# Seven block products for eight in the second load of each token-major group, in a two-layer fp32 trunk

## The chip, the cores and the metric

The kernel runs on one core of one Trainium2 chip. The core has five engines with a queue each: TensorE (PE, matrix multiplication, whose loading of stationary blocks is listed as PEld), VectorE (DVE), ScalarE (ACT), GpSimd (POOL) and SyncE (SP, which here issues the loads). PE writes its sums to eight PSUM banks of 128 x 512 fp32. The metric is the device time of one execution in microseconds (us); the median over runs is compared.

## The reference

256 tokens of width 2048 pass through an mLSTM layer and a differential-attention layer, each followed by a gated feed-forward part with a short convolution, then a last RMS norm. Weights and sums are float32. Cut to its products, with `rms_norm`, gates and softmax as their names say:

```python
# layer 0
proj = rms_norm(h, a_norm) @ w_in                 # 2048 -> q 1024, k 1024, v 2048, o 2048, gates 16
hm = mlstm_chunkwise(q, k, v, i_pre, log_f)       # 8 heads, v of width 256 a head
h = h + (rms_norm(hm, w_hnorm) * sigmoid(o)) @ w_out             # 2048 x 2048
h = h + conv_ffn(rms_norm(h, f_norm[0]), w_up, ..., w_down)      # 2048 -> 2 x 5632 -> 2048
# layer 1
k, v = split(rms_norm(h, kv_norm) @ w_kv)         # 2048 -> 2048 + 2048, k rotated
q = rotated(rms_norm(h, b_norm) @ w_q)
pd = softmax(q1 k1) - lam * softmax(q2 k2)        # causal, 8 heads
h = h + (rms_norm(pd @ v, subln) * (1 - lambda_init)) @ w_o      # 2048 x 2048
h = h + conv_ffn(rms_norm(h, f_norm[1]), w_up, ..., w_down)
return rms_norm(h, final_norm)
```

## The kernel before, in words

**Products in halves.** Every fp32 operand is split in a high part h (a copy rounded by ACT to the type PE reads) and a low part l (the rest, by DVE); a product is three matmuls, xh wh + xl wh + xh wl. Weights come as loads of 1 MB, four k-tiles of 128 rows by 512 columns, into four slots ("raw"). Half a load at a time ACT makes h (line 376) and DVE l (line 377), into one of five slots ("w2"). Activations are split once, when they are made.

**Token-major products.** v, o, w_out, attention v, w_o and w_down have tokens on the output's partitions. `gemm_tokens` (products on line 437) goes through groups of 512 columns; a group has 16 k-tiles (w_down more) and two PSUM banks, a for tokens 0 to 127 and b for 128 to 255. Two k-tiles are 12 matmuls of 128x512 (columns of weights moving past a stationary 128x128 block of x). After the last k-tile `evac` takes the banks.

**Seven products for eight.** `gemm_sevenths` (products on line 493) treats one load of a group, at the k-tile named in `at`, otherwise: two k-tiles, two halves of tokens and two halves of columns form a 2 x 2 product of blocks, which Strassen's scheme in Winograd's form makes with seven block products in place of eight. A block product is three matmuls of 128x256, so four k-tiles take 42 of these in place of 24 of 128x512. The scheme needs differences of weight blocks (`sevenths`, lines 449 to 451, into a "raw" slot), seven blocks split rather than four (lines 458 and 459, tiles of 3 x 256 and 4 x 256 columns), mixtures of the x blocks (`mix`, lines 531 to 537; `mix_again` for x that was split before, its first step on line 551), and sums of the products: some go straight into a and b, the rest into two further banks c and d, which are added up at the end of the group, by `mixed_up` (lines 559 to 565) into a and b, or by `mixed_in` (lines 572 to 579) into the residual stream. The remaining k-tiles of the group are plain (line 503).

Before the change that load is the third of the group (k-tile 8, `OUT_AT`), and seven groups have it: o 1 and 2, w_out 1 to 3, w_o 2 and 3. All groups of v and attention v are plain. w_down has its own places (`MIXED`).

**Banks.** Four of the eight banks are the pool `acc_ps`, which holds a and b of two successive groups; four are `sm_ps`, for all small products (scores, values, turns, columns of parameters) and, before, for c and d.

**What sets the order.** The code runs once and records instructions; a list scheduler then gives each engine its queue, by priority in program order and its own idea of what is ready. `tick()` stands after each two k-tiles, and `later(n, f)` puts f after n further ticks: so the small work of a head is spread between the large products. In attention, the keys of the eight heads come from a product by pairs of k-tiles; after each head's keys `rotated` (lines 936 to 941) multiplies and rotates them on DVE and POOL, `softmax` makes the scores on PE (955 to 957), maxima (959), exponentials and the weights `pc` (966 to 970), and `turned` transposes them on PE (977) for ACT and DVE to split (`pt`, 321 and 323). The last heads' part of this falls into the first groups of attention v. In mLSTM the same holds of `weights`, `values` and `scaled`; there the norm's inverse root is computed by POOL in 12 small instructions (lines 279 to 282), and ACT's scaling on line 348 waits for it.

## Time and profile before

| | |
|---|---|
| median of 3 runs | 2253.62 us (2253.61 to 2253.67) |
| profiled execution | 2253.21 us |
| span of its instructions | 2251.4 us |
| PE busy | 2239.6 us (99%) |
| DVE busy | 1789.7 us (79%) |
| ACT busy | 1292.0 us (57%) |
| POOL busy | 125.0 us (6%) |
| DMA | 419.04 MB, 186 GB/s over the span |

All durations come from the profiled execution. Rows of groups read: line, engine, operation, written tile <- read tiles, shape, number; then busy time in all in us, mean of one in ns, and the engine's idle time just before them with what ended it. Rows of the timeline give start and length in us, both from the span's start. Rows of waits give who waited for whom: us in all, times, longest. The row "PEclk" gives the clock granted to PE in tenths, in 40 slices of the span.

### The profile page before, as it was taken

To read this page: it belongs to the slowest core of one execution; us is meant where nothing else is said; L and a number is where in the kernel's file an instruction comes from. 1 tells how busy PE (TensorE), PEld (TensorE's weight loads), DVE (VectorE), ACT (ScalarE), POOL (GpSimd) and SP (SyncE) were. 2 spreads that over 40 slices of the span, in tenths; PEclk is the share of its full clock that TensorE was granted. 3 is DMA by queue.
4 is the path that set the end of the run, shared out by engine and by line. 5 is a ranking of instruction groups with operands and counts; after the bars stand their busy time and mean duration, and the time that the engine had idled before them with its cause. 6 is when DMAs were issued, how large, how long until landed. Compare 5 with 4: busy or idle time off the path is not lost.

```text
span 2251.4 us, 33430 instructions
## 1 busy us (share of the span) xinstructions
PE 2239.6 (99%) x12843; PEld 1954.1 (87%) x12843; DVE 1789.7 (79%) x2964; ACT 1292.0 (57%) x1994; POOL 125.0 (6%) x305
## 2 busy tenths in 40 slices
PE   9999999999999999999999999999999999999998
PEld 9888888888888888888888888888888888888888
DVE  5756778887888877879998885677877988778896
ACT  5456655655555555656654556566555555556554
POOL 0014200000000000000022103200000000000000
PEclk9999999999999999999999999999999999999999
DMA  7554546555555755545566555465555457555464
GB/s 265 188 169 157 166 171 205 192 191 187 187 170 179 242 187 187 187 150 203 189 208 194 163 167 169 150 206 187 187 187 187 156 191 239 191 189 191 146 215 150
DMA packets 325348, 419.04 MB, mean 186 GB/s; under 512 B 9070, under 2 KB 238788, under 8 KB 325188
## 3 DMA queue, kind: packets, MB, share of 16 engines
q1 hardware_dynamic: 325156, 416.89, 56.4%
q8 instruction: 101, 1.65, 0.3%
q14 instruction: 59, 0.48, 0.1%
q10 hardware_dynamic: 32, 0.01, 0.0%
HBM read 414.77 MB, written 2.10 MB: 185 GB/s over the span
## 4 chain that ended last, share of the span: by engine, by line
PE 97%; DVE 1%; POOL 1%; issue 1%; ACT 0%; DMA 0%; DVEq 0%; SPq 0%; POOLq 0%
PE acc L411 54%; PE acc L503 16%; PE acc L437 12%; PE mix L493 6%; PE acc L493 4%; PE acc L634 2%; PE acc L521 1%; PE val_ps L335 1%; PE turn_ps L231 1%; PE as_ps L955 0%; DVE w L377 0%; POOL rs_u L279 0%; POOL rs_u L280 0%; DMA pos_i<-in_positions_dram 0%; POOL rs_u L281 0%
## 5 line engine op out<-in xcount | busy, mean ns | idle before, releaser
L377 DVE TENSOR_TENSOR w<-raw,w 128x1024 fp32r<-128x1024 f32 x679 | 825.9, 1220 | 280.1 <-ACT w L376 277.5
L376 ACT ACTIVATE w<-raw 128x1024 fp32r<-128x1024 f32 x679 | 713.9, 1058 | 491.7 <-PE acc L411 324.8
L411 PE MATMUL acc<-x_f,w 128*128 128x512 f32 (+1 forms) x5632 | 988.1, 337 | 0.0
L411 PEld LDWEIGHTS acc<-x_f,w 128*128 128x128 f32 x5632 | 861.7, 188 | 123.2
L503 PE MATMUL acc<-w,hid 128*128 128x512 f32 x1080 | 268.2, 394 | 0.0
L503 PEld LDWEIGHTS acc<-w,hid 128*128 128x128 f32 x1080 | 195.4, 188 | 39.0
L411 PE MATMUL acc<-x_at,w 128*128 128x512 f32 (+1 forms) x1024 | 182.1, 338 | 0.0
L411 PEld LDWEIGHTS acc<-x_at,w 128*128 128x128 f32 x1024 | 156.8, 188 | 22.2 <-issue 0.3
L458 ACT ACTIVATE w<-diff 128x1024 fp32r<-128x1024 f32 x89 | 94.1, 1057 | 111.1 <-DVE diff L451 81.7
L417 ACT ACTIVATE low<-acc 128x256 f32<-128x256 f32 x216 | 79.3, 386 | 135.4 <-PE acc L411 132.6
L459 DVE TENSOR_TENSOR w<-diff,w 128x1024 fp32r<-128x1024 f32 x89 | 108.7, 1221 | 40.9 <-ACT w L458 40.3
L437 PE MATMUL acc<-w,x_a 128*128 128x512 f32 x576 | 138.0, 396 | 0.0
L437 PEld LDWEIGHTS acc<-w,x_a 128*128 128x128 f32 x576 | 106.8, 188 | 24.2
L493 PE MATMUL mix<-w,mix 128*128 128x256 f32 x801 | 119.3, 281 | 0.0
L418 DVE TENSOR_TENSOR acc<-acc,low 128x256 f32<-128x256 f32 x216 | 84.5, 430 | 37.7 <-ACT low L417 37.3
L493 PEld LDWEIGHTS mix<-w,mix 128*128 128x128 f32 x801 | 107.0, 188 | 2.4 <-DVE w L459 0.2
L848 ACT ACTIVATE c<-u,conv 128x256 f32<-128x256 f32 x176 | 98.2, 593 | 5.5 <-DVE u L846 5.2
L939 POOL TENSOR_TENSOR sw<-sw,sin_t 32x256 f32<-32x256 f32 x32 | 42.0, 1328 | 1033.8 <-DVE sw L938 1022.5
L458 ACT ACTIVATE w<-raw 128x768 fp32r<-128x768 f32 x89 | 74.7, 840 | 37.9 <-PE acc L503 27.4
L437 PE MATMUL acc<-w,x_at 128*128 128x512 f32 x384 | 91.8, 396 | 0.0
L459 DVE TENSOR_TENSOR w<-raw,w 128x768 fp32r<-128x768 f32 x89 | 84.6, 951 | 2.8 <-ACT w L458 2.7
L493 PE MATMUL acc<-w,hid 128*128 128x256 f32 x450 | 86.3, 281 | 0.0
(302 smaller groups left out, 2320.4 us busy)
## 6 DMA issues: line engine op xcount, KB each, us to landing
raw<-in_w_up_dram SPq DMA_DIRECT2D x176, 1024.0 KB
raw<-in_w_down_dram SPq DMA_DIRECT2D x79, 1024.0 KB
raw<-in_m_w_in_dram SPq DMA_DIRECT2D x46, 1024.0 KB
raw<-in_w_kv_dram SPq DMA_DIRECT2D x32, 1024.0 KB
raw<-in_m_w_out_dram SPq DMA_DIRECT2D x16, 1024.0 KB
raw<-in_w_q_dram SPq DMA_DIRECT2D x16, 1024.0 KB
raw<-in_w_o_dram SPq DMA_DIRECT2D x16, 1024.0 KB
raw<-in_w_down_dram SPq DMA_DIRECT2D x15, 512.0 KB
```

The source lines that it names most:

```text
L376: act.activation(w2[:, :hc, 0], part, AF.Copy)
L377: dve.tensor_tensor(w2[:, :hc, 1], part, w2[:, :hc, 0].bitcast(F32), op=ALU.subtract)
L411: pe.matmul(to, a, b, start=(k == 0 and o == 0), stop=(k == kn - 1 and o == len(ops) - 1))
L417: act.activation(low, p[:, T:], AF.Copy)
L418: dve.tensor_tensor(p[:, :T], p[:, :T], low, op=ALU.add)
L437: pe.matmul(ps[t], a[:, s], b, start=(k == 0 and o == 0), stop=(k == kn - 1 and o == 2))
L458: act.activation(w2[:, :m, 0], src, AF.Copy)
L459: dve.tensor_tensor(w2[:, :m, 1], src, w2[:, :m, 0].bitcast(F32), op=ALU.subtract)
L493: pe.matmul(to, u, v, start=start and o == 0, stop=end and o == 2 and to is not a and to is not b, skip_group_check=True)
L503: pe.matmul(ps, u[:, s], v, start=(k0 + i == 0 and o == 0), stop=(k0 + i == kn - 1 and o == 2), skip_group_check=True)
L634: pe.matmul(ps[j], a, b, start=(k == 0 and o == 0 and j % 2 == 0), stop=(k == KD - 1 and o == 2), skip_group_check=True)
L848: act.activation(c, u, AF.Identity, bias=cw[:, 3, f:f + 1], scale=cw[:, 2, f:f + 1])
```

## The change

Five things, in 18 groups now: all of mLSTM v, mLSTM o, w_out and attention v, and groups 2 and 3 of w_o.

- `OUT_AT` is (4, 6): the load with seven products is the second of the group (k-tiles 4 to 7).
- v, all of o, group 0 of w_out and attention v use `gemm_sevenths`. For v and o the mixtures of x are made ahead of v rather than ahead of o; attention v makes its own from its normed x.
- With the new argument `mid`, c and d come from `acc_ps`.
- Directly behind the products of that load, within the group, `mid` adds them up: `mixed_in` into the residual stream, or `mixed_sums` into two SBUF tiles.
- At the end of the group `mixed_up` adds these tiles to a and b, two additions of 128x512. `mixed_up` before did both steps at the end.

w_down keeps its scheme, with c and d in `sm_ps`.

```diff
--- before.py
+++ after.py
@@ -37,7 +37,7 @@
 G = 512
 NG = D // G
 RAW = 4
-OUT_AT = (8, 10)
+OUT_AT = (4, 6)
 MIXED = (4, 12, 20)
 HL = 5
 WARM, WARM_X = 28, 24
@@ -461,7 +461,8 @@
             pairs.append(out)
         return pairs
 
-    def gemm_sevenths(xs, mixed, w, col0, groups, evac, at):
+    def gemm_sevenths(xs, mixed, w, col0, groups, evac, at, mid=None):
+
 
 
         kn, raws = len(xs), {}
@@ -472,7 +473,10 @@
             while k0 < kn:
                 if k0 in at:
                     if c is None:
-                        c, d = small_ps("mix"), small_ps("mix")
+                        if mid is None:
+                            c, d = small_ps("mix"), small_ps("mix")
+                        else:
+                            c, d = (acc_ps.tile([P, 2 * T], F32, tag="acc", name="mix") for _ in range(2))
                     parts = sevenths(w, col0 + g * G, k0, min(2, (kn - k0) // 2))
                     for p, (b1, b2, b3, t1, t3, t2, t4) in enumerate(parts):
                         k = k0 + 2 * p
@@ -493,6 +497,8 @@
                                 pe.matmul(to, u, v, start=start and o == 0, stop=end and o == 2 and to is not a and to is not b, skip_group_check=True)
                         if p < len(parts) - 1:
                             tick()
+                    if mid is not None and k0 == at[-1]:
+                        sums = mid(g, (c, d))
                     k0 += 4
                 else:
                     for i, (wh, wl) in enumerate(granule(w, col0 + g * G, G, k0, kn, raws, g)):
@@ -503,7 +509,7 @@
                                 pe.matmul(ps, u[:, s], v, start=(k0 + i == 0 and o == 0), stop=(k0 + i == kn - 1 and o == 2), skip_group_check=True)
                     k0 += 2
                 tick()
-            evac(g, (a, b), (c, d))
+            evac(g, (a, b), (c, d) if mid is None else sums)
 
     def gemm_by_tokens(xs, w, col0, evac):
 
@@ -551,9 +557,9 @@
             dve.tensor_tensor(c, h.bitcast(F32), l.bitcast(F32), op=ALU.add)
         return mix(pair)
 
-    def mixed_up(ps, mix):
-
-        (a, b), (c, d) = ps, mix
+    def mixed_sums(g, mix):
+
+        c, d = mix
         u = tmp("mx")
         x, y = block(F32, "mixed_a"), block(F32, "mixed_b")
         act.activation(x[1], c[:, :T], AF.Copy)
@@ -561,8 +567,11 @@
         dve.tensor_tensor(y[1], d[:, T:], u, op=ALU.add)
         dve.tensor_tensor(x[0], d[:, :T], u, op=ALU.add)
         dve.tensor_tensor(y[0], d[:, :T], y[1], op=ALU.add)
-        dve.tensor_tensor(a, a, x[2], op=ALU.add)
-        dve.tensor_tensor(b, b, y[2], op=ALU.add)
+        return x[2], y[2]
+
+    def mixed_up(ps, sums):
+        for p, x in zip(ps, sums):
+            dve.tensor_tensor(p, p, x, op=ALU.add)
 
     def mixed_in(g, mix):
 
@@ -748,7 +757,8 @@
             for n in range(2):
                 dve.tensor_tensor(k[2 * j + n], ps[n], norm.r, op=ALU.mult)
 
-        def evac_v(g, ps):
+        def evac_v(g, ps, sums):
+            mixed_up(ps, sums)
             for c in range(2):
                 h = 2 * g + c
                 v[h] = [scaled_split(ps[t][:, c * VD:(c + 1) * VD], norm.rt[:, t:t + 1], f"mv{h}_{t}", T + 2) for t in range(2)]
@@ -794,9 +804,8 @@
         def scaled(h, banks, y):
             hn[h] = normed_rows(banks, y, block(F32, f"hn{h}")[:2])
 
-        def evac_o(g, ps, mix=None):
-            if mix is not None:
-                mixed_up(ps, mix)
+        def evac_o(g, ps, sums):
+            mixed_up(ps, sums)
             for c in range(2):
                 h, rows = 2 * g + c, []
                 for t in range(2):
@@ -823,12 +832,10 @@
         dve.tensor_scalar(rt_half, norm.rt, 0.5, None, op0=ALU.mult)
         gates()
         gemm(xs, w, HQK, range(4), evac_k)
-        gemm_tokens(xs, w, 2 * HQK, range(4), evac_v)
+        x_mixed = {k: mix_again(xs[k], xs[k + 1]) for k in OUT_AT}
+        gemm_sevenths(xs, x_mixed, w, 2 * HQK, range(4), evac_v, OUT_AT[:1], mixed_sums)
         later_parameters_in()
-        x_mixed = {k: mix_again(xs[k], xs[k + 1]) for k in OUT_AT}
-        gemm_tokens(xs, w, 2 * HQK + HV, [0], evac_o)
-        gemm_sevenths(xs, x_mixed, w, 2 * HQK + HV, [1, 2], evac_o, OUT_AT[:1])
-        gemm_tokens(xs, w, 2 * HQK + HV, [3], evac_o)
+        gemm_sevenths(xs, x_mixed, w, 2 * HQK + HV, range(4), evac_o, OUT_AT[:1], mixed_sums)
         return outs, outs_mixed
 
 
@@ -977,7 +984,8 @@
                 pe.transpose(t_ps[:, d * P:(d + 1) * P], p[:, s * P:(s + 1) * P], ident)
             pt[h] = split_weights(t_ps, h, "pt")
 
-        def evac_v(g, ps):
+        def evac_v(g, ps, sums):
+            mixed_up(ps, sums)
             for c in range(2):
                 h = 2 * g + c
                 v = [scaled_split(ps[t][:, c * VD:(c + 1) * VD], norm.rt[:, t:t + 1], f"av{h}_{t}") for t in range(2)]
@@ -1010,7 +1018,9 @@
 
         gemm(norm.sets[0], w_q[0], 0, range(8), evac_q_and_operands)
         gemm(norm.sets[1], w_kv, 0, range(8), rotated(k, "ak", softmax))
-        gemm_tokens(norm.sets[1], w_kv, AQK, range(4), evac_v)
+        xs = norm.sets[1]
+        x_mixed = {k: mix_again(xs[k], xs[k + 1]) for k in OUT_AT}
+        gemm_sevenths(xs, x_mixed, w_kv, AQK, range(4), evac_v, OUT_AT[:1], mixed_sums)
         return outs, outs_mixed
 
     convs, later_layers = [], []
@@ -1036,16 +1046,14 @@
 
     outs, outs_mixed = mlstm(norm_a)
     norm_f0 = Norm([(gains, G_F0)], "f0")
-    gemm_tokens(outs, m_w_out[0], 0, [0], residual(norm_f0))
-    gemm_sevenths(outs, outs_mixed, m_w_out[0], 0, range(1, NG - 1), residual(norm_f0), OUT_AT[:1])
-    gemm_sevenths(outs, outs_mixed, m_w_out[0], 0, [NG - 1], residual(norm_f0), OUT_AT[:1])
+    gemm_sevenths(outs, outs_mixed, m_w_out[0], 0, range(NG), residual(norm_f0), OUT_AT[:1], mixed_in)
 
     norm_at = Norm([(gains, G_B), (gains, G_KV)], "at")
     conv_ffn(0, norm_f0, residual(norm_at))
     outs, outs_mixed = attention(norm_at)
     norm_f1 = Norm([(gains, G_F1)], "f1")
     gemm_tokens(outs, w_o[0], 0, range(2), residual(norm_f1), lead=2)
-    gemm_sevenths(outs, outs_mixed, w_o[0], 0, range(2, NG), residual(norm_f1), OUT_AT[:1])
+    gemm_sevenths(outs, outs_mixed, w_o[0], 0, range(2, NG), residual(norm_f1), OUT_AT[:1], mixed_in)
 
 
     norm_out = Norm([], "out")
```

**Where instructions stand.** PE at the beginning of attention v, before: the turn of one head's weights (t_ps, from pc, which DVE writes), the scores of the next head (as_ps), then wide products of group 0.

```order
L977 MATMUL t_ps_12748<-ident_109,pc_12628 128x128 [waits DVE_49]
L977 MATMUL t_ps_12748<-ident_109,pc_12628 128x128 x2
L955 MATMUL as_ps_12759<-ak6_12693,aq6_11657 128x256 [waits PE_49]
L956 MATMUL as_ps_12759<-ak6_12693,aq6_11657 128x128
L957 LDWEIGHTS ident_b_118
L957 MATMUL as_ps_12759<-mask_a_127,ident_b_118 128x256
L955 MATMUL as_ps_12769<-ak6_12693,aq6_11657 128x256 [waits PE_49,Activation_49]
L956 MATMUL as_ps_12769<-ak6_12693,aq6_11657 128x128
L957 LDWEIGHTS ident_b_118
L957 MATMUL as_ps_12769<-mask_a_127,ident_b_118 128x256
L437 MATMUL acc_12844<-w2_12863,x_at_3_11138 128x512 x2
L437 MATMUL acc_12845<-w2_12863,x_at_3_11138 128x512 x3
```

What follows until the next turn is products of group 0 alone. After the change the part from the end of that head's scores to the next turn reads, whole:

```order
L964 MATMUL as_ps_13047<-mask_a_127,ident_b_118 128x256
L497 MATMUL acc_13149<-w2_13237,x_at_7_11630 128x256 [waits Activation_49]
L497 MATMUL acc_13149<-w2_13237,x_at_7_11630 128x256
L497 MATMUL acc_13149<-w2_13237,x_at_7_11630 128x256 [waits DVE_49]
L509 MATMUL acc_13149<-w2_13292,x_at_8_11734 128x512 [waits Activation_49]
L509 MATMUL acc_13149<-w2_13292,x_at_8_11734 128x512
L509 MATMUL acc_13149<-w2_13292,x_at_8_11734 128x512 [waits DVE_49]
L509 MATMUL acc_13149<-w2_13292,x_at_9_11737 128x512 x3
L497 MATMUL mix_13220<-w2_13228,x_at_4_11520 128x256 [waits DVE_49,PE_49]
L497 MATMUL mix_13220<-w2_13228,x_at_4_11520 128x256 x2
L984 MATMUL t_ps_13182<-ident_109,pc_13044 128x128 [waits DVE_49]
```

Six matmuls of 128x256 and six of 128x512 stand now between a head's scores and the turn of the weights that DVE computes from them.

DVE in the same head, before, from the second product of the keys (ak7) with the norm to the factor of the second softmax:

```order
L936 TENSOR_TENSOR ak7_12831<-acc_12707,rstd_at_10988 128x256
L938 STREAM_SHUFFLE sw_12833<-ak7_12831 32x256 [waits DVE_49]
L938 STREAM_SHUFFLE sw_12839<-ak7_12831 32x256 [waits DVE_49]
L940 TENSOR_TENSOR ak7_12831<-ak7_12831,cos_t_2256 32x256 [waits DVE_49]
L966 RECIPROCAL l_12758<-l_12758 128x4 [waits Activation_49]
L940 TENSOR_TENSOR ak7_12831<-ak7_12831,cos_t_2256 32x256 [waits DVE_49]
L967 TENSOR_SCALAR l_12758<-l_12758,neg_lam_2607 128x2 [waits DVE_49]
```

and after, from the same instruction on:

```order
L943 TENSOR_TENSOR ak7_13109<-acc_12985,rstd_at_11266 128x256
L945 STREAM_SHUFFLE sw_13111<-ak7_13109 32x256 [waits DVE_49]
L945 STREAM_SHUFFLE sw_13117<-ak7_13109 32x256 [waits DVE_49]
L557 TENSOR_TENSOR mx_13122<-x_at_4_11520 128x256
L557 TENSOR_TENSOR mx_13123<-x_at_5_11523 128x256
L557 TENSOR_TENSOR mx_13135<-x_at_6_11627 128x256
L557 TENSOR_TENSOR mx_13136<-x_at_7_11630 128x256
L947 TENSOR_TENSOR ak7_13109<-ak7_13109,cos_t_2422 32x256 [waits DVE_49]
L973 RECIPROCAL l_13036<-l_13036 128x4 [waits Activation_49]
L947 TENSOR_TENSOR ak7_13109<-ak7_13109,cos_t_2422 32x256 [waits DVE_49]
L539 TENSOR_TENSOR sum_13126<-mx_13122 128x128 [waits DVE_49]
L537 TENSOR_TENSOR sum_13126<-mx_13122,mx_13123 128x128 [waits DVE_49]
```

The additions that recombine x (line 557, four) and the first of eight small ones of `mix` stand now between the steps of the head.

## The prediction, on record before the result

> **What bounds the kernel now.** I read the page's engine table first, then the chain that ended last, then the waits of TensorE (PE).
>
> ```profile
> PE 2239.6 (99%) x12843; PEld 1954.1 (87%) x12843; DVE 1789.7 (79%) x2964; ACT 1292.0 (57%) x1994; POOL 125.0 (6%) x305
> PEclk9999999999999999999999999999999999999999
> PE 97%; DVE 1%; POOL 1%; issue 1%; ACT 0%; DMA 0%; DVEq 0%; SPq 0%; POOLq 0%
> PE warm_ps L130 <- DVE warm L126: 1.0, 1, 1.0
> PE lam_ps L916 <- ACT hn L348: 0.7, 1, 0.7
> ```
>
> PE is busy for 99% of the span, holds 97% of the last chain, at a full clock; the view of its waits has five rows, 1.0 us the longest. So a matmul less is time less, as long as PE is never kept waiting, and almost any stall is new time. DVE is the next busiest engine at 79%; the change gives it work, so its share must be read stage by stage.
>
> ```profile
> core 0: us, PE busy (x) PEld busy (x) DVE busy (x) ACT busy (x) POOL busy (x), PEclk, DMA share, GB/s
> 107.80:208.90 101.10, 101.10 (x475) 83.49 (x474) 59.78 (x111) 57.30 (x113) 27.07 (x100) 1.00 0.52 170
> 208.90:305.40 96.50, 95.46 (x481) 79.42 (x480) 75.35 (x143) 59.27 (x100) 19.20 (x44) 1.00 0.53 178
> 305.40:328.60 23.20, 23.20 (x106) 18.86 (x105) 16.77 (x26) 12.76 (x19) 0.00 (x0) 1.00 0.40 136
> 328.60:351.20 22.60, 22.60 (x124) 19.32 (x123) 16.13 (x22) 13.28 (x19) 0.00 (x0) 1.00 0.49 167
> 1036.70:1066.80 30.10, 30.10 (x187) 26.81 (x186) 28.36 (x38) 19.56 (x28) 0.00 (x0) 1.00 0.53 181
> 1318.50:1420.40 101.90, 101.90 (x490) 84.19 (x489) 63.89 (x114) 58.40 (x116) 21.89 (x70) 1.00 0.52 166
> ```
>
> These are, in order, the windows of mLSTM v, mLSTM o, a plain group of w_out, a group of w_out with the seven products, a group of w_down, and attention v. In the w_down row DVE is busy 28.36 of 30.10 us, 94%, and PE is busy throughout: a full DVE alone costs nothing, provided that what PE asks for stands early enough in DVE's order.
>
> **The gain.** Seven groups have the load with seven products before, eighteen after: eleven more. In each, 24 matmuls of 128x512 become 42 of 128x256.
>
> ```profile
> 1036.86 5.59 PE acc L503 x24
> 2227.45 15.63 PE acc L521 x132
> ```
>
> Rows of the chain: 5.59/24 = 0.2329 us for the wide matmul, 15.63/132 = 0.1184 for the narrow. 24 x 0.2329 - 42 x 0.1184 = 0.62 us a group, and the two w_out windows show it directly: 23.20 - 22.60 = 0.60. Eleven groups at 0.61: **-6.7 us**.
>
> **The load on DVE.** Prices by form:
>
> ```profile
> L377 DVE TENSOR_TENSOR w<-raw,w 128x1024 fp32r<-128x1024 f32 x678 | 825.2, 1221 | 280.1 <-ACT w L376 277.5
> L459 DVE TENSOR_TENSOR w<-diff,w 128x1024 fp32r<-128x1024 f32 x89 | 108.7, 1221 | 40.9 <-ACT w L458 40.3
> L459 DVE TENSOR_TENSOR w<-raw,w 128x768 fp32r<-128x768 f32 x89 | 84.6, 951 | 2.8 <-ACT w L458 2.7
> L449 DVE TENSOR_TENSOR diff<-raw 128x1024 f32<-128x1024 f32 x37 | 45.1, 1219 | 4.2 <-DMA raw<-in_w_down_dram 3.3 <-DMA raw<-in_w_o_dram 0.8
> L450 DVE TENSOR_TENSOR diff<-raw,diff 128x512 f32<-128x512 f32 x37 | 25.3, 684 | 0.1
> L560 DVE TENSOR_TENSOR mx<-mix,mixed_a 128x256 f32<-128x256 f32 x2 | 0.8, 414 | 0.0
> L564 DVE TENSOR_TENSOR acc<-acc,mixed_a 128x512 f32<-128x512 f32 x2 | 1.4, 686 | 0.0
> L551 DVE TENSOR_TENSOR mx<-x_a 128x256 f32<-128x256 f32 x4 | 1.5, 405 | 0.0
> L537 DVE TENSOR_TENSOR mix<-sum,mix 128x512 fp32r<-128x512 f32 x26 | 17.8, 684 | 0.0
> L531 DVE TENSOR_TENSOR sum<-mx 128x128 f32<-128x128 f32 x6 | 1.7, 282 | 0.1
> ```
>
> An added group in v or o costs DVE: differences 1.219 + 2 x 0.684 = 2.59; four splits 2 x 1.221 + 2 x 0.951 = 4.34 in place of two, 2.44; sums 4 x 0.414 = 1.66; adds into the banks 2 x 0.686 = 1.37. Net 7.5 us. The two mixings of x cost 2 x (2 x 0.405 + 4 x 0.282 + 0.684) = 5.2 us; attention pays them anew, mLSTM already had them. So DVE comes to 59.8 + 30.1 = 90 of 98.7 us in mLSTM v (91%), about 75.4 + 15.0 - 5.2 = 85 of 95 in o (89%), 63.9 + 30.1 = 94 of 99.5 in attention v (94%). None is over its window. The mixings lie just ahead of the groups. In w_out and w_o DVE has a quarter of the time free (16.77 of 23.20), and the sums there only move: cost nothing, and if that cover failed, their 1.7 to 3 us in one group. The load on ACT grows by four copies and a split, from 58.4 of 101.9: nothing.
>
> **Where the order bites: the first group of attention v.** The orders above show it. A head's attention is a loop over two engines: PE turns the weights of one head (t_ps) and makes the scores of the next (as_ps); DVE takes maxima, rotates the following head's keys and ends with pc; PE turns that pc.
>
> ```profile
> 1318.53 4.58 PE L437 MATMUL acc<-w,x_at 128*128 128x512 f32 x19
> 1322.95 0.49 PE L977 MATMUL t_ps<-ident,pc 128*128 128x128 f32 x3
> 1324.72 11.64 PE L437 MATMUL acc<-w,x_at 128*128 128x512 f32 x49
> 1336.21 0.49 PE L977 MATMUL t_ps<-ident,pc 128*128 128x128 f32 x3
> 1307.44 1.20 DVE L377 TENSOR_TENSOR w<-raw,w 128x1024 fp32r<-128x1024 f32 x1
> 1309.59 1.23 DVE L377 TENSOR_TENSOR w<-raw,w 128x1024 fp32r<-128x1024 f32 x1 [0.95 <-ACT w L376]
> 1322.68 1.23 DVE L377 TENSOR_TENSOR w<-raw,w 128x1024 fp32r<-128x1024 f32 x1 [1.04 <-ACT w L376]
> 1329.84 1.21 DVE L377 TENSOR_TENSOR w<-raw,w 128x1024 fp32r<-128x1024 f32 x1
> 1330.97 0.41 DVE L941 TENSOR_TENSOR ak<-ak,sw 32x256 f32<-32x256 f32 x1
> 1331.31 0.73 DVE L970 SCALAR_TENSOR_TENSOR pc<-pc,l 128x256 f32<-128x256 f32 x2
> ```
>
> Before, the loop takes 1331.31 + 0.73 - 1322.95 = 9.1 us from turn to pc, and PE asks for pc 13.3 us after the first turn, since 49 matmuls stand between: 4.2 us to spare. In the changed order only these stand between the two turns: the first turn and its scores (1324.72 - 1322.95 = 1.8 us), six narrow matmuls and six wide (0.7 + 1.4): 3.9 us. DVE's part loses one split (1329.84 to 1330.97, 1.1 us) and gains eight small instructions of the mixing, which stand inside the head's own tail: 4 x 0.405 + 4 x 0.282 = 2.75, or 2.2 as instructions in a row overlap by 0.07 us. The loop takes 9.1 - 1.1 + 2.2 = 10.2 us, and PE stands still 10.2 - 3.9 = **6.3 us**.
>
> A second way counts DVE's own backlog. From the end of the stage's first split (1308.64) to pc (1332.04) DVE now needs 23.4 us, 2.0 of them idle in the two bracketed waits. After the change the differences (2.59) stand ahead of that split, some 1.0 in idle time; then come six splits as before, two of them smaller (-0.5), the mixing (2.2), and 1.0 us of the head before. So pc comes at 1308.6 + 1.6 + 21.4 + 2.7 = 1334.3 without idle time, 1336.3 with all of it. PE asks at 1318.53 + 30 x 0.2329 + 12 x 0.1184 + 1.8 = 1328.7: a stall of 5.6 to 7.6. I take **+6.5**, within both. While PE stands, DVE and ACT go on with the next splits, so the 94% behind it starts with a lead; I add nothing for the other three groups.
>
> **mLSTM v and o.** The trace has no group of v with seven products. From below: 96.50 - 95.46 = 1.04 us that PE idles in o today may vanish, since products leave the small banks that the conv columns and scores share. From above, ACT:
>
> ```profile
> 144.49 1.19 POOL L280 TENSOR_TENSOR rs_u<-rs_u,den 128x2 f32<-128x2 f32 x1
> 146.04 0.20 POOL L282 TENSOR_TENSOR yh<-yh,rs_u 128x2 f32<-128x2 f32 x1
> ACT hn L348 <- POOL yh L282: 14.7, 6, 4.2
> ```
>
> ACT waits six times for a chain of small POOL instructions, 2.45 us on average and 4.2 at worst, and its copies for the splits queue behind. Two-operand POOL instructions of one size take 0.20 or 1.19 us. If a fuller DVE made each such wait the worst one and no lead of the splits were left, every one of o's four groups would lose 4.2 - 2.45 = 1.75: 7.0 us. The w_down window is the nearest row, a fuller DVE at no cost, so I take **+1.0**, near the lower end.
>
> The Trainium skill (SBUF — State Buffer, "Who interferes with whom") speaks against the change here: a DVE instruction with two SBUF operands holds a port pair that GpSimd needs, for its whole length. The trace agrees as far as the 1.19 us beside the 0.20 go; taken to its end the rule gives the 7.0 us above.
>
> **Sum.** 2253.2 (profiled) - 6.7 + 6.5 + 1.0 = 2254.0; the median of the runs, 2253.6, stands 0.4 above the profiled execution: **2254.4 us**.
>
> **Rivals.** (1) Faster: the loop in attention v doesn't stall, because DVE reaches the head's tail with maxima and rotation done sooner than I read, and PE's idle 1.0 in o goes: 2253.6 - 6.7 - 1.0 = 2245.9. For it: DVE idles 2.0 us in that stretch, and PE has almost no waits now. Against it: the 3.9 us of PE's work in the loop stand fixed in its order, and DVE's tail alone was 9.1 us. It counts as faster, under 2249.1, if all stalls together are under 2.2 us. (2) Slower: ACT behind POOL's chain in mLSTM o, at 7.0 us, with the loop's 6.5: 2253.6 - 6.7 + 6.5 + 7.0 = 2260.4. It decides from stalls over 11.2 us in all. For it: DVE at 89 to 91% there, and 4.2 us waits already seen. Against: only 1.04 us reach PE today. (3) Bank wait: products now take banks that the former group's evacuation must free; 24 wide matmuls (5.6 us) stand ahead of the first product, so an evacuation later than that costs its excess. With DVE at 94%, one excess of 2 us in attention v gives 2256.4, inside the likeliest case's range; DVE's backlog of about a head's tail (9.1 - 5.6 = 3.5 us) in each of three groups would give 2264.9.
>
> **How the numbers follow.** 0.2%, 4.5 us, is about what a measurement can tell from no change. Likeliest: gain and stall nearly cancel, 57% (2249.1 to 2258.1, with 5 to 7.6 for the loop, the ends of mLSTM and a small bank wait). Faster case 18%, slower cases (2) and the large (3) together 25%. The range for 8 in 10 runs from 2248.0, a little into case 1, to 2262.0, past case 2.
>
> **What would show it.** The waits of PE should have one row for the turn (t_ps on DVE's pc) of about 6 us, near 1330; the w_out groups should all last about 22.6 us; the matmuls saved should take PE's busy time down by 6 to 7 us; DVE should be over 90% busy in attention v. I am wrong if the turn's wait is under 2 us, if waits for products' banks or for splits in v and o exceed it, or if the added matmuls of 128x256 average above 0.12 us.

## The result, and the profile after

The changed kernel takes **2292.47 us** (median of 6 runs, 2290.73 to 2293.93) against 2253.64 us before (2253.29 to 2254.19): a ratio of 1.0172, 95% interval 1.0159 to 1.0185. It is 38.8 us slower. The forecast was 2254.4 in a range of 2248.0 to 2262.0, with a chance of 25% for slower: the time lies far outside.

The page of the changed kernel, engine table, clock and one group of matmuls:

```profile
span 2290.7 us, 34047 instructions
PE 2244.9 (98%) x13041; PEld 1967.0 (86%) x13041; DVE 1862.4 (81%) x3099; ACT 1308.4 (57%) x2029; POOL 139.1 (6%) x305
PEclk9999899999999999999999999999999999999999
L509 PE MATMUL acc<-w,x_a 128*128 128x512 f32 x576 | 147.0, 407 | 17.4 <-DVE mx L566 16.2
```

On the page of the kernel before, a group of as many matmuls of that shape, those of the plain groups of v and o:

```profile
L437 PE MATMUL acc<-w,x_a 128*128 128x512 f32 x576 | 138.0, 396 | 0.0
```

The span grew by 39.3 us. PE's idle time grew by 34.0 of them (11.8 to 45.8). Its busy time should have fallen by 6.7 and rose by 5.3 (2239.6 to 2244.9), so matmuls cost 12.0 us more than their number says. The fifth digit of the clock is an 8 now, and the 576 matmuls of 128x512 in the two rows above, equal in number and shape, cost 9.0 us more. Where the idle time lies is in the waits of PE, after (us in total, times, longest):

```profile
PE acc L509 <- DVE mx L566: 16.2, 3, 9.3
PE val_ps L335 <- issue: 7.3, 2, 5.9
PE t_ps L984 <- DVE pc L977: 6.2, 1, 6.2
```

The third row is the stall in attention v that the prediction worked out as 6.3 us (the place where PE waits for a head's weights `pc`). The first is none of its terms: the first matmul of a group waits for line 566, the first of the *sums* of the group before. By stage, each from its first large product to that of the next, in the changed kernel (mLSTM v and o together, w_out, attention v, w_o; columns as in the prediction's windows):

```profile
109.45:336.42 226.97, 201.18 (x1060) 170.33 (x1059) 172.92 (x322) 127.56 (x232) 51.45 (x144) 0.95 0.45 150
336.42:426.54 90.12, 90.12 (x490) 77.41 (x488) 75.85 (x103) 52.52 (x76) 0.00 (x0) 1.00 0.60 202
1350.55:1458.67 108.12, 101.06 (x561) 87.17 (x560) 93.07 (x182) 66.16 (x135) 31.14 (x69) 0.97 0.52 166
1458.67:1552.81 94.14, 94.14 (x477) 78.90 (x476) 67.65 (x94) 53.22 (x92) 12.28 (x39) 1.00 0.54 179
```

and before:

```profile
107.76:305.39 197.63, 196.59 (x952) 162.94 (x951) 135.12 (x253) 116.61 (x211) 46.26 (x144) 1.00 0.53 174
305.39:396.32 90.93, 90.93 (x471) 76.80 (x470) 69.52 (x95) 51.74 (x76) 0.00 (x0) 1.00 0.54 182
1318.53:1420.36 101.83, 101.83 (x489) 84.12 (x488) 63.82 (x114) 58.37 (x116) 21.85 (x70) 1.00 0.52 166
1420.36:1512.64 92.28, 92.28 (x467) 77.12 (x466) 64.04 (x88) 53.70 (x88) 11.93 (x37) 1.00 0.51 171
```

mLSTM v and o went from 197.6 to 227.0 us, **+29.3**. w_out, with one more group of seven products and the same sums moved, went down by 0.8. Attention v and w_o together went from 194.1 to 202.3, +8.2. The stretch ahead of v, where the mixing of x stands now, and the feed-forward part of layer 0 are each 1.7 longer; the rest is 0.8 shorter. So three quarters of the loss lie in mLSTM v and o, where the prediction had +1.0 beside the saving.

**What PE waits for in mLSTM v and o.** PE's timeline of the changed kernel has the longest stalls there and, last, that of attention v (start, duration, work, in brackets the idle time before it and its releaser):

```profile
182.19 3.02 PE L509 MATMUL acc<-w,x_a 128*128 128x512 f32 x12 [0.70 <-DVE den L794]
210.73 3.04 PE L509 MATMUL acc<-w,x_a 128*128 128x512 f32 x12 [0.97 <-DVE mx L566]
...
240.40 1.20 PE L335 MATMUL val_ps<-mv,st 128*128 128x258 f32 x4 [5.86 <-issue]
...
280.68 5.26 PE L509 MATMUL acc<-w,x_a 128*128 128x512 f32 x12 [9.29 <-DVE mx L566]
...
311.67 5.13 PE L509 MATMUL acc<-w,x_a 128*128 128x512 f32 x12 [5.95 <-DVE mx L566]
...
1368.08 0.90 PE L984 MATMUL t_ps<-ident,pc 128*128 128x128 f32 x3 [6.16 <-DVE pc L977]
```

Take the stall of 9.29 us ahead of o's third group. The second group's products end at 265.8. Line 566 needs ACT's copy of bank c (line 565), and ACT does in the meantime:

```profile
276.13 0.84 ACT L348 ACTIVATE hn<-val_ps,yh 128x256 f32<-128x256 f32 x2 [3.86 <-POOL yh L282]
...
277.89 0.84 ACT L306 ACTIVATE mo<-hn_ps,half_h 128x256 fp32r<-128x256 f32 x2 [0.55 <-DVE mo L307]
...
279.68 0.38 ACT L565 ACTIVATE mixed_a<-mix 128x256 f32<-128x256 f32 x1
...
308.08 0.84 ACT L550 ACTIVATE mx<-hn_ps,half_h 128x256 f32<-128x256 f32 x2 [1.06 <-DVE mo L307]
309.93 0.63 ACT L542 ACTIVATE mix<-sum 128x512 fp32r<-128x512 f32 x1 [1.01 <-DVE sum L540]
310.46 0.36 ACT L565 ACTIVATE mixed_a<-mix 128x256 f32<-128x256 f32 x1
```

The copy comes 13.9 us after the last product (279.68 - 265.81), behind the output of two heads (hn, mo). In the next group, the last three rows, it comes 15.9 us after it (310.46 - 294.55), behind the mixing of the heads' output for w_out. Neither has to do with the sums; they merely stand ahead of them in ACT's order (for hn, ACT itself waits 3.86 us on POOL). The banks c and d stay taken for that long, and the next group's own sums a and b need them. ACT's order in that place, cut, shows it (3267 to 3273 are splits of the *next* group, 3118 is the copy):

```
L458 ACTIVATE w2_3267<-raw_3261 128x3x256 [waits DMAHW1_49,PE_49,Activation_49]
L458 ACTIVATE w2_3270<-diff_3263 128x4x256 [waits DVE_49,PE_49,Activation_49]
L542 ACTIVATE mix_3012<-sum_3007 128x512 [waits DVE_49]
L306 ACTIVATE mo6_3021<-hn_ps_3016,half_h_145 128x256
L458 ACTIVATE w2_3273<-raw_3261 128x3x256 [waits PE_49,Activation_49]
...
L550 ACTIVATE mx_3028<-hn_ps_3016,half_h_145 128x256 [waits DVE_49]
L542 ACTIVATE mix_3036<-sum_3031 128x512 [waits DVE_49]
L565 ACTIVATE mixed_a_3118<-mix_3055 128x256
```

Counted in matmuls behind the group's last product, the copy stands at 14, 19, 48, 48 in the four groups of v, at 48, 43, 51, 26 in those of o, and at 18 to 20 in the first three of attention v. Behind these products a group still has 48 wide matmuls, so a copy that stands fewer than 48 behind can still come before the next group begins. The place alone does not give the length of a stall: the copy at 43 is the one ahead of the 9.29 us, and ACT waits for POOL on the way to it.

A tag names a set of buffers ("slots") of a pool that all tiles of that tag share. The pattern fits one rule: in the whole order the tiles of one tag are first written in the sequence in which the program recorded their first writes. The sums' tiles (`mixed_a`, `mixed_b`, and `mx` from the tag of the temporaries) were recorded behind tiles of the heads that share their tags, so the copy may not come before those have been written. That is **theory A**: the place in the queue of slots, not the work, delays the sums.

**Theory B**, the rival, blames POOL. One two-operand instruction on 128x2, 0.20 us in its next occurrence, lasts 8.86 us here:

```profile
225.17 8.86 POOL L280 TENSOR_TENSOR rs_u<-rs_u,den 128x2 f32<-128x2 f32 x1
...
234.94 0.20 POOL L280 TENSOR_TENSOR rs_u<-rs_u,den 128x2 f32<-128x2 f32 x1
```

It is the chain whose end ACT's hn waits for, and behind hn stands the `st` that PE's matmul at 240.40 takes in. ACT's timeline there:

```profile
236.82 0.84 ACT L348 ACTIVATE hn<-val_ps,yh 128x256 f32<-128x256 f32 x2 [8.54 <-POOL yh L282]
...
239.88 0.62 ACT L321 ACTIVATE st<-wt 128x256 fp32r<-128x256 f32 x2 [0.66 <-DVE wt L784]
```

So 8.54 us of waiting (4.2 at worst before) stand ahead of the stall of 5.86. Under B the fuller DVE starves POOL, POOL holds ACT, and the sums are late with everything else.

### The profile page after: what moved, and what is told of

Same layout as the page of the kernel before. It is cut to its first block, busy times and chain, and to the rows that moved or that the text cites. A ratio compares the mean times of both kernels' runs of the same rounds, so it can differ in the third digit from the quotient of the medians.

```text
span 2290.7 us, 34047 instructions
## 1 busy us (share of the span) xinstructions
PE 2244.9 (98%) x13041; PEld 1967.0 (86%) x13041; DVE 1862.4 (81%) x3099; ACT 1308.4 (57%) x2029; POOL 139.1 (6%) x305
## 4 chain that ended last, share of the span: by engine, by line
PE 91%; DVE 4%; POOL 2%; issue 1%; ACT 1%; DMA 1%; SPq 0%; DVEq 0%; ACTq 0%; POOLq 0%
PE acc L411 52%; PE acc L509 21%; PE mix L497 6%; PE acc L497 4%; PE acc L437 3%; PE acc L643 2%; DVE w L377 1%; POOL rs_u L280 1%; PE acc L527 1%; PE turn_ps L231 1%; PE val_ps L335 1%; POOL rs_u L281 0%; POOL yh L282 0%; DVE w L459 0%; POOL rs_u L279 0%
## 5 line engine op out<-in xcount | busy, mean ns | idle before, releaser
L377 DVE TENSOR_TENSOR w<-raw,w 128x1024 fp32r<-128x1024 f32 x657 | 798.2, 1221 | 222.5 <-ACT w L376 220.2
L376 ACT ACTIVATE w<-raw 128x1024 fp32r<-128x1024 f32 x657 | 687.8, 1058 | 465.8 <-PE acc L411 330.4
L458 ACT ACTIVATE w<-diff 128x1024 fp32r<-128x1024 f32 x111 | 117.4, 1057 | 148.3 <-DVE diff L451 86.5
L459 DVE TENSOR_TENSOR w<-diff,w 128x1024 fp32r<-128x1024 f32 x111 | 135.8, 1223 | 70.9 <-ACT w L458 70.3
L509 PE MATMUL acc<-w,x_a 128*128 128x512 f32 x576 | 147.0, 407 | 17.4 <-DVE mx L566 16.2
L497 PE MATMUL mix<-w,mix 128*128 128x256 f32 x999 | 147.9, 282 | 0.0
L497 PEld LDWEIGHTS mix<-w,mix 128*128 128x128 f32 x999 | 132.5, 189 | 2.4 <-DVE w L459 0.2
L458 ACT ACTIVATE w<-raw 128x768 fp32r<-128x768 f32 x111 | 93.4, 841 | 54.4 <-PE acc L509 41.1
L418 DVE TENSOR_TENSOR acc<-acc,low 128x256 f32<-128x256 f32 x216 | 84.4, 430 | 40.6 <-ACT low L417 40.4
L459 DVE TENSOR_TENSOR w<-raw,w 128x768 fp32r<-128x768 f32 x111 | 105.8, 954 | 10.2 <-ACT w L458 10.1
L857 DVE SCALAR_TENSOR_TENSOR c<-u,conv,c 128x254 f32<-128x254 f32 x176 | 78.9, 480 | 1.3
```

The lines of the kernel that those rows point to most:

```text
L376: act.activation(w2[:, :hc, 0], part, AF.Copy)
L377: dve.tensor_tensor(w2[:, :hc, 1], part, w2[:, :hc, 0].bitcast(F32), op=ALU.subtract)
L418: dve.tensor_tensor(p[:, :T], p[:, :T], low, op=ALU.add)
L458: act.activation(w2[:, :m, 0], src, AF.Copy)
L459: dve.tensor_tensor(w2[:, :m, 1], src, w2[:, :m, 0].bitcast(F32), op=ALU.subtract)
L497: pe.matmul(to, u, v, start=start and o == 0, stop=end and o == 2 and to is not a and to is not b, skip_group_check=True)
```

## The experiments

All twelve compute the whole reference. The time of each is compared with that of the kernel before on the same chip (2253.4 to 2253.7 us). The diffs are against the changed kernel.

**1. The sums' tiles in slots of their own** (theory A alone):

```diff
+    def own(name):
+        b = work.tile([P, 2 * T], F32, tag="sums", name=name, bufs=2)
+        return b[:, :T], b[:, T:], b
-        return work.tile([rows, T], dt, tag="tmp", name=name, bufs=8)
+        return work.tile([rows, T], dt, tag="tmp", name=name, bufs=4)
-        u = tmp("mx")
-        x, y = block(F32, "mixed_a"), block(F32, "mixed_b")
+        x, y = own("mixed_a"), own("mixed_b")
+        u = y[0]
-        u = block(F32, "mixed")
+        u = own("mixed")
```

> The changed kernel, with one thing different: the tiles for the sums (mixed_a, mixed_b, and mixed for w_out) have two slots of their own instead of coming from the pool of 49 blocks that the heads' tiles use; to make room the temporaries have 4 slots for 8, and the sum's intermediate sits in mixed_b. In the order the copy mixed_a then stands 5 to 20 matmuls behind the last product in every group, where it stood 43 to 51 behind it in groups 2 to 6 of mLSTM v and o. Theory A (a tile's first write stands in the order behind those of all tiles of its pool that were recorded before it, so the sums wait for the heads' work, and the next group waits for their banks): the three waits 'acc <- mx', 16.2 us, and the slower matmuls behind them, some 5 us, go: 2292.5 - 21 = about 2271. Theory B (ACT's queue stands behind the root that POOL computes, and POOL is kept from working by an unbroken row of DVE instructions): the waits for mx only turn into waits for splits or values; 2284 to 2292.

**2. The heads' reciprocal root on DVE** (theory B alone):

```diff
-            y = rsqrt(d, "yh", pool)
+            y = rsqrt(d, "yh", dve)
```

> The changed kernel with one thing different: in mLSTM the inverse root of a head's norm is computed by DVE (9 instructions of 128x2) instead of POOL (12). Theory A: the sums keep their place in the order, 44 to 51 matmuls late in most groups, so the waits for mx stay near 16 us; only the waits for values (7.3 us) go: about 2283. Theory B: the waits for values (7.3) and the longest wait for mx (9.3, behind ACT's hn) go with the slow matmuls behind them: about 2270. The wait for mx of 5.95 us in front of the last group of o, where POOL does nothing, stays under both.

**3. Both together:**

> Both edits of the two runs before at once. If A and B are separate causes, the gains add: the waits for mx and for values both go, leaving the wait of attention v's turn (6.2 us and its slow matmuls) against 6.7 us fewer matmul time: 2253 to 2260. If B alone is the cause, as the run with the root on DVE; if A alone, as the run with own slots.

**4. Attention v plain again**, all else as changed:

```diff
-        x_mixed = {k: mix_again(xs[k], xs[k + 1]) for k in OUT_AT}
-        gemm_sevenths(xs, x_mixed, w_kv, AQK, range(4), evac_v, OUT_AT[:1], mixed_sums)
+        gemm_tokens(xs, w_kv, AQK, range(4), evac_v)
```

> The changed kernel with the four groups of attention v plain again (no seven products, no mixing of x there). Takes away the turn's wait of 6.2 us, the wait of 0.7 and the slower matmuls behind (3.5 us by the windows of attention v and w_o), gives back 4 x 0.61 = 2.4 us of saved matmuls: 2292.5 - 6.9 - 3.5 + 2.4 = about 2284.5. If the turn's wait were hidden by something else, or stays because DVE is late for another reason: 2292 to 2295.

Measured: 2274.66 us (2273.93 to 2275.37; ratio 1.0094, 1.0079 to 1.0109) with own slots; **2304.51** (1.0225, 1.0208 to 1.0243) with the root on DVE; 2276.59 (1.0102, 1.0087 to 1.0117) with both; 2286.84 (1.0148, 1.0132 to 1.0163) with attention v plain.

Own slots give 17.8 of the 38.8 us back, 4 us less than A said and far more than B did. The copy stands at 14, 19, 16, 16 and 16, 20, 20, 20 matmuls behind the products of v and o, and the waits of PE, here with own slots, have no row for the sums:

```profile
PE t_ps L988 <- DVE pc L981: 6.2, 1, 6.2
PE acc L513 <- ACT w L380: 3.3, 3, 1.5
PE an_ps L361 <- ACT nrm L352: 1.7, 1, 1.7
PE w_ps L778 <- ACT hn L352: 1.7, 1, 1.7
```

mLSTM v and o are 24.1 us shorter than in the changed kernel; attention v is 2.4 longer. Windows of the two with own slots:

```profile
109.58:312.47 202.89, 194.36 (x1053) 164.54 (x1052) 169.21 (x318) 127.06 (x231) 40.23 (x144) 1.00 0.50 164
1327.21:1437.70 110.49, 101.86 (x546) 86.86 (x547) 92.17 (x181) 64.10 (x130) 33.76 (x68) 0.95 0.47 153
```

The root on DVE is a miss for both theories: it makes the kernel 12 us slower still. Its waits of PE:

```profile
PE acc L509 <- DVE mx L566: 13.6, 4, 6.9
PE val_ps L335 <- issue: 12.7, 2, 8.9
```

The waits for the sums stay near A's 16 us, and the one of 5.95 us ahead of o's last group, where POOL does nothing, is there unchanged; the longest falls from 9.3 to 6.9 us, which may be POOL's share in it. The wait that B should have removed (val_ps) grows from 7.3 to 12.7 us. DVE's timeline of that kernel shows the root's steps ahead of the longer of the two:

```profile
233.48 0.14 DVE L275 TENSOR_TENSOR rs_u<-yh 128x2 f32<-128x2 f32 x1
233.55 3.48 DVE L377 TENSOR_TENSOR w<-raw,w 128x1024 fp32r<-128x1024 f32 x3
...
237.90 0.14 DVE L276 SCALAR_TENSOR_TENSOR rs_u<-rs_u,den 128x2 f32<-128x2 f32 x1
```

The steps of the root stand in DVE's order with three splits and 4.3 us between two of them. In DVE's own queue, too, other work stands between the steps of the root. So the experiment does not clear POOL; it shows that moving the chain is no cure. With own slots the root's engine makes 2 us (2274.66 and 2276.59, where 2253 to 2260 was expected of both edits together). Only the heads of mLSTM had their root moved; whether POOL is part of what is left is not shown by it.

Attention v plain gives back 5.6 us and its t_ps row is gone; 8 were expected. PE idles no more in attention v and the stage itself is 8.0 us shorter (100.08 for 108.12), but w_o behind it takes 1.4 longer.

**5. The mixing of x for attention v earlier** (with own slots): its two combinations are issued at the start of the keys' product instead of behind it.

```diff
-        gemm(norm.sets[1], w_kv, 0, range(8), rotated(k, "ak", softmax))
-        x_mixed = {k: mix_again(xs[k], xs[k + 1]) for k in OUT_AT}
+        x_mixed = {}
+        for n, i in enumerate(OUT_AT):
+            later(2 + 4 * n, lambda i=i: x_mixed.update({i: mix_again(xs[i], xs[i + 1])}))
+        gemm(norm.sets[1], w_kv, 0, range(8), rotated(k, "ak", softmax))
```

> The kernel with own slots for the sums, and the mixing of x for attention v recorded early in the product of the keys (2 and 6 granules behind its start) instead of at its end. In the order PE then has 10.7 us of its own work between the last two turns of a head's weights, where it had 3.1; the eight small DVE instructions of the mixing no longer stand in the head's tail. Theory of the loop (PE to DVE to PE: 9 to 10 us against the work that PE has in between): the turn's wait (6.2 us) goes, and the slow matmuls behind it; attention v and w_o together come from 206 us to about 193: 2262. Rival (DVE, over 90% busy in attention v, is the bound there, wherever the turn stands): other waits of the same size appear in attention v, 2270 to 2275.

**6. The first group of attention v plain, the mixing behind it** (with own slots):

```diff
+        gemm_tokens(xs, w_kv, AQK, [0], evac_v)
-        gemm_sevenths(xs, x_mixed, w_kv, AQK, range(4), evac_v, OUT_AT[:1], mixed_sums)
+        gemm_sevenths(xs, x_mixed, w_kv, AQK, range(1, 4), evac_v, OUT_AT[:1], mixed_sums)
```

> The kernel with own slots for the sums, with the first group of attention v plain and the mixing of x recorded behind it; groups 1 to 3 keep the seven products. PE has 12 to 17 us of work between turns. Theory of the loop: no wait for the turn, three groups save 3 x 0.61 = 1.8 us: attention v and w_o together 194.1 - 1.8 = 192.3, the whole 2274.7 - 13.6 = 2261. Rival (DVE is the bound in attention v): waits for splits or banks in groups 1 to 3, 2268 to 2275.

Measured: 2265.58 (2264.02 to 2266.78; 1.0054, 1.0037 to 1.0071) with the early mixing, 2271.61 (2270.39 to 2272.82; 1.0079, 1.0064 to 1.0094) with a plain first group. By the order, an estimate, 10.7 us of PE's work stand between the last two turns of the heads' weights in the first, 12 and more in the second, 3.1 in the changed kernel and 12 to 13 before. The wait for pc is gone in both. Attention v with the early mixing:

```profile
1326.76:1428.10 101.34, 99.57 (x547) 84.47 (x547) 86.98 (x166) 62.74 (x129) 25.40 (x57) 1.00 0.53 171
```

101.3 for 110.5 us with own slots alone. So undoing the loop over two engines gives 9.2 us, not only the 6.2 of its row: 6.9 us of idle time and 2.3 of PE's busy time. (The edit changes both sides of the loop, PE's work between the turns and DVE's work in the head's tail; which of them does more is not shown.) With a plain first group the stage still takes 107.9, and the time falls into the range of the rival, 2268 to 2275. But the waits are not those that it named, splits or banks, and DVE is busy for only 84.4 of the 107.9 us. PE waits for `an_ps` on ACT's nrm, 5.4 us in three waits, and ACT's nrm on POOL's root, 16.2 us in four. So with the loop gone ACT behind POOL's chain shows in attention v; no run moved that root.

**7. Banks c and d from the small pool again**, the sums still taken within the group:

```diff
-                        if mid is None:
-                            c, d = small_ps("mix"), small_ps("mix")
-                        else:
-                            c, d = (acc_ps.tile([P, 2 * T], F32, tag="acc", name="mix") for _ in range(2))
+                        c, d = small_ps("mix"), small_ps("mix")
```

> The changed kernel with one thing different: the products' two banks come from the four small banks again, as before the change; the sums are still taken within the group, into blocks. In the order the sums stay late (28 to 78 matmuls behind the last product in most groups of mLSTM v and o). Theory A: late sums cost only since the next group's first matmul needs their banks, so the waits 'acc <- mx' (16.2 us) go: 2265 to 2275. Rival (a late sum or ACT's queue hurts whatever bank it holds): 2285 to 2295; and if the heads' small products miss the two banks, waits for values, scores and turns take their place, also over 2280.

Measured: **2297.34** (1.0194, 1.0179 to 1.0209), slower than the changed kernel. Its waits of PE:

```profile
PE acc L506 <- ACT w L376: 9.9, 12, 1.2
PE t_ps L981 <- DVE pc L974: 7.5, 1, 7.5
...
PE w_ps L771 <- ACT hn L348: 2.9, 1, 2.9
PE cols_ps L1040 <- ACT hn L348: 2.6, 1, 2.6
```

The wait for mx goes with the large banks, but other waits take its place, the largest of them for ACT's splits. The late copies hold small banks now, which the heads' scores and columns need (w_ps and cols_ps); that this is what delays them is a reading, not shown. Theory A as I had put it for this run, 2265 to 2275, was wrong by 22 us; the rival, over 2280, held.

**8. Own slots, with mLSTM v and attention v plain** (10 groups of seven products are left: four of o, four of w_out, two of w_o):

> The kernel with own slots for the sums, and v and attention v plain again, so that o, w_out (four groups each) and w_o (two) have the seven products: three groups more than before the change. If what is left of the loss with own slots (5.3 us in mLSTM v and o, 12 in attention v and w_o) comes from DVE's work in v and attention v: 2253.6 - 3 x 0.61 = 2251.8. If the own slots, with 4 temporaries for 8, cost something by themselves (w_out is 1.2 us longer in that run): 2253 to 2257.

Measured: 2260.34 (2259.69 to 2260.99, 7 runs; 1.0029, 1.0018 to 1.0040), 3 us above the nearer of the two expectations. mLSTM v and o take 200.88 us, 6.57 idle, most of it just behind the edge from v to o (stalls of 3.1 and 1.7 us at 219.6 and 224.8), where the rotary tables, the mixing for o and the first group fall together:

```profile
108.12:309.00 200.88, 194.31 (x980) 162.38 (x979) 147.85 (x279) 120.42 (x219) 47.38 (x144) 1.00 0.49 161
```

**9. The slots as in the changed kernel, but taken early.** Own slots changed the pools too (half the small tiles, more room for the sums). This one leaves the pools alone: the sums' three tiles are taken at the start of the group, and POOL clears one column of each.

```diff
+            tiles = (tmp("mx"), block(F32, "mixed_a"), block(F32, "mixed_b")) if mid is mixed_sums else None
+            for t in tiles or ():
+                pool.memset((t[2] if type(t) is tuple else t)[:, :1], 0.0)
-                        sums = mid(g, (c, d))
+                        sums = mid(g, (c, d), tiles) if tiles else mid(g, (c, d))
```

> The changed kernel, pools as they are, with one addition: the three tiles of the sums (mx, mixed_a, mixed_b) are taken at the start of each group and POOL writes one column of each with zeros there. That makes their first write stand ahead of the heads' tiles of that group; the copy mixed_a then stands 12 to 20 matmuls behind the last product (36 in the last group of o) where it stood 43 to 51 behind. If the order of first writes within a pool is the cause (theory A), this does what the own slots did: the waits 'acc <- mx' under 2 us in all, about 2270 to 2277. If it was the smaller number of temporaries or the own slots themselves that helped: near 2292.

**10. The same with the early mixing of attention v:**

> The run before, with the mixing of x for attention v recorded early in the product of the keys. Theory A and the theory of the loop add: the run before less 9 us, about 2262 to 2267. If temporaries (8 here, 4 with own slots) are what holds mLSTM v back, it comes out some 5 us under the run with own slots and early mixing (2265.6).

Measured: 2273.46 (2272.74 to 2276.12; 1.0090, 1.0076 to 1.0104) and 2262.75 (2261.04 to 2264.47; 1.0040, 1.0026 to 1.0054), both within what A gives. The copy stands at 14, 19, 16, 16 and 12, 20, 20, 36 matmuls behind the products. Taking the same tiles early *without* a write leaves the order as it was in the changed kernel (built, not timed): it is the first write that holds the place. mLSTM v and o with the tiles written early:

```profile
109.06:316.01 206.95, 198.65 (x1060) 168.36 (x1059) 171.68 (x321) 126.99 (x231) 37.14 (x162) 0.98 0.50 164
```

20.0 us shorter than in the changed kernel, with the same pools, the same banks, the same matmuls and the same work on DVE and ACT; POOL even has 18 instructions more in the window. Theory A holds. Nor do the fewer temporaries of the own slots hold mLSTM back: with 8 of them, (10) takes 207.4 us there and (5), with 4, 202.8. That POOL is busy 37.1 us here for 51.5, with more to do, fits its being starved less as well, but as a consequence: the root stayed on POOL.

**11 and 12. What can be kept.** Own slots; plain: v and o's first group. Seven products: o's other three groups, w_out's four and w_o's two. In the first of the two also attention v's four, with the early mixing; in the second attention v is plain.

```diff
-        gemm_sevenths(xs, x_mixed, w, 2 * HQK, range(4), evac_v, OUT_AT[:1], mixed_sums)
+        gemm_tokens(xs, w, 2 * HQK, range(4), evac_v)
-        gemm_sevenths(xs, x_mixed, w, 2 * HQK + HV, range(4), evac_o, OUT_AT[:1], mixed_sums)
+        gemm_tokens(xs, w, 2 * HQK + HV, [0], evac_o)
+        gemm_sevenths(xs, x_mixed, w, 2 * HQK + HV, range(1, 4), evac_o, OUT_AT[:1], mixed_sums)
```

> Own slots for the sums; v plain, o plain in its first group and seven products in the other three, w_out all four, attention v all four with the mixing recorded early in the product of the keys, w_o two: 13 groups against 7 before. Saved: 6 x 0.61 = 3.7 us. If the loss in mLSTM v and o comes from the sevenths' DVE work at the edge from v to o (rotary tables, mixing of x and the first group of o at one place): under 2 us is lost there, 3.5 us in attention v as in the run with early mixing: 2253.6 - 3.7 + 2 + 3.5 = 2255. If own slots with 4 temporaries cost by themselves: 2259 to 2262.

> As the run before, with attention v plain: 9 groups against 7 before, 1.2 us saved. If only the edge from v to o cost in the run with all of o (2260.3): 2252.4 to 2254. If own slots with 4 temporaries cost by themselves: 2257 to 2260.

Measured: 2256.09 (2254.54 to 2258.07, 11 runs; 1.0010, 1.0001 to 1.0019) and 2256.93 (2255.29 to 2260.58, 11 runs; 1.0017, 1.0008 to 1.0026). The first is about as expected. The second is 3 us above its first expectation and at the edge of the other, that own slots with 4 temporaries cost by themselves (2257 to 2260), which is so not excluded. mLSTM v and o of the second, and its longest waits:

```profile
108.24:305.14 196.90, 195.81 (x971) 163.54 (x969) 141.80 (x267) 117.72 (x216) 45.82 (x144) 1.00 0.51 166
```

```profile
PE cols_ps L1046 <- ACT hn L352: 1.1, 1, 1.1
PE warm_ps L134 <- DVE warm L130: 1.0, 1, 1.0
```

There is no loss left in v and o (197.6 before), and attention v takes 100.2 us without idle time. In the profiled execution the last stage, from the first product of the second feed-forward part to the end, is 2.4 us longer than before (741.2 for 738.8), though its products are the same. The own slots and the four temporaries hold there too, but in (11), which has the same ones, it takes 738.0. Why is not settled. No version beats the kernel before, so the groups of seven products added in the heads' stages have, in every version run, cost at least what they save.

| kernel | us | mLSTM v and o: us, PE idle | attention v: us, PE idle |
|---|---|---|---|
| before | 2253.64 | 197.6, 1.0 | 101.8, 0 |
| changed | 2292.47 | 227.0, 25.8 | 108.1, 7.1 |
| own slots (1) | 2274.66 | 202.9, 8.5 | 110.5, 8.6 |
| own slots, early mixing (5) | 2265.58 | 202.8, 8.4 | 101.3, 1.8 |
| written early (9) | 2273.46 | 207.0, 8.3 | 110.7, 9.5 |
| written early, early mixing (10) | 2262.75 | 207.4, 8.3 | 101.4, 1.7 |
| own slots, v and attention v plain (8) | 2260.34 | 200.9, 6.6 | plain: 100.3, 0 |
| own slots, o's last three, early mixing (11) | 2256.09 | 198.9, 1.5 | 101.7, 2.0 |
| own slots, o's last three, attention v plain (12) | 2256.93 | 196.9, 1.1 | plain: 100.2, 0 |

## Why the prediction was wrong

**The gain was right.** In w_out's stage one group more, with the sums moved, saved 0.8 us against 0.6 forecast; PE's added narrow matmuls run at the old price (999 of `mix` in 147.9 us, 801 in 119.3 before: 0.148 and 0.149 each on the pages). So the 6.7 us may be taken as saved and lost elsewhere. What did not come is the fall of PE's busy time by 6 to 7 us: slower matmuls, most of them behind the stalls, hide it. DVE over 90% busy in attention v did not come either: its 93.1 us are those forecast, but in a stage of 108.1 they are 86%.

**The loop in attention v was right in place, but its cost was priced too low.** Forecast: 6.3 us by the loop, 5.6 to 7.6 by the backlog, on `t_ps` for `pc`. Measured: 6.16 us, that row. That it came so close is in part luck: from the turn at 1356.86 to pc at 1368.03 the loop took 11.2 us where 10.2 stood, and PE had 4.4 us of its own work and a wait of 0.7 in that time where 3.9 stood. Undoing it (5) gave the stage 9.2 us back, 2.3 of them busy time of PE, in part matmuls that run slowly behind the stall (below). A term of about 9 where 6.5 stood.

**w_out and w_o were right.** "The sums there only move: cost nothing": w_out is full at 1.00 clock without idle time. The copies are late there too, 29 to 38 matmuls behind the products in the order, but the rest of the group still covers them: the first comes at 352.15, 4.4 us behind the products, and the next group begins some 11 us behind them. w_o is 1.9 us longer by its window, but the window holds all 144 of its wide matmuls now and held 136 before; the other 8, 1.9 us at 0.233, stood behind the first product of the next stage.

**The step that failed is mLSTM v and o**: +1.0 us, with bounds of -1.0 and +7.0. The stages lost 29.3 us, and 3.7 more that six groups should have saved: 33. The error is not only of size but of mechanism. The upper bound came from one wait already in the trace, ACT behind POOL's chain, multiplied by its worst case. The text counted how much work DVE and ACT had gained, found none over its window, and never looked up in the changed order *where* the new copy stands on ACT. It stands 43 to 51 matmuls behind the products, with the next group's splits and two heads' output ahead of it; a load of 91% or 56% says nothing on that. The same reading of the order, done for one place in attention v, gave the one stall that came out. Of the 33 us, the copy's place in the order makes 20 to 24 (runs 9 and 1). The other 9 to 13 are not taken apart: with own slots PE still idles 8.5 us there, 3.3 of them for ACT's splits, 1.7 for hn and the rest in smaller waits.

**Rival (3) had the right resource and the wrong side.** It asked whether the *evacuation* frees the products' banks in time and priced an excess over 5.6 us of wide matmuls. But the group's own a and b take banks at its very start, with nothing ahead of them, and what frees those is the sums of the group before. Rival (2), ACT behind POOL's chain, shows up (`hn` on `yh` 20.4 us for 14.7, one instruction of 8.86 us) and stands ahead of the stall of 5.86 us at 240.40, which no run isolated; with the slots apart, the engine of the root makes 2 us. Its price rested on two-operand POOL instructions of "0.20 or 1.19 us"; the trace before already had one of that size at 2.29 us (line 280 at 213.29) and one at 3.04 (line 279 at 231.85). For rival (1) nothing in the runs speaks.

POOL's 8.86 us themselves go further than the 1.19 us on which the prediction leaned. DVE's timeline of the changed kernel, first and last row of that time, between which no row has idle time:

```profile
225.28 1.21 DVE L377 TENSOR_TENSOR w<-raw,w 128x1024 fp32r<-128x1024 f32 x1
...
233.57 0.41 DVE L906 SCALAR_TENSOR_TENSOR ang<-turns,ang 32x256 f32<-32x256 f32 x1
```

POOL's instruction began at 225.17 and ended at 234.03, 0.05 us behind the last of these eleven. The Trainium skill (SBUF — State Buffer, "Who interferes with whom") has the shared port pair as an exclusive lock. The trace fits a lock, and adds that POOL did not get in for 8.86 us while DVE's instructions followed each other without a gap. It does not show the lock itself: one of the eleven (line 776, 0.41 us) reads one of its two operands from PSUM, and POOL's instruction did not end behind that one either.

What stays open, beside the 9 to 13 us above: the 3 us that (12) lies above its expectation, and how the 6.6 us idle of (8) at the edge of v and o are shared among the tables, the mixing and the first group; (12) shows only that without the first group they are gone.

## What to carry to other kernels

When an instruction is added that frees a scarce buffer, read its place in the engine's scheduled order, not the engine's load: ask what stands ahead of it, and what the buffer's next user has ahead of itself. In the orders built here, tiles that share a tag are first written in the sequence in which the program records those writes, so a short-lived tile in a tag shared with another pipeline inherits that pipeline's delays; give it a tag of its own, or write it early. And price a long stall of PE above its own length: behind every stall of 5.9 us and more in these runs the matmuls ran slowly for a while.
